# A 128-byte unused tile between the activation tiles and the weight tiles of a two-layer decoder trunk

## The chip, the cores and the metric

The kernel runs on one core of a Trainium2 chip. The metric is the device time of one execution in microseconds (us); lower is better.

## The reference

Two decoder layers work on 512 tokens of width 1024 in float32. Each has three sub-layers, each with a normalisation before and after it and a residual sum:

```
for l in range(DEPTH):
    h = hybrid_mixer(rmsnorm(x, pre_mix_g[l]), ...)          # dilated attention + mLSTM, one w_in, one w_out
    x = x + rmsnorm(h, post_mix_g[l])
    h = memory_cross_attention(rmsnorm(x, pre_mem_g[l]), mem, wq, wk, wv, wo)
    x = x + rmsnorm(h, post_mem_g[l])
    h = conv_ffn(rmsnorm(x, pre_ffn_g[l]), w_up, conv_w, conv_b, w_down)   # 1024 -> 2*2816 -> 1024
    x = x + rmsnorm(h, post_ffn_g[l])
```

Nearly all the arithmetic is in the products of activations with weights: w_in, w_out, the four projections of the cross-attention, w_up and w_down.

## The kernel before

**Split products.** Every float32 operand of a large product is split into a high and a low part (`split` L93, `load_unit` L84), and a product is three matmuls (`mm3` L108): high by high, high by low, low by high. Each matmul loads one stationary operand of 128 columns (512 bytes per partition) and streams a moving operand past it, mostly 512 columns (2,048 bytes per partition), into one accumulator in PSUM. Each matmul in the program has a weight load of its own, which the trace shows as PEld.

**The operands.** Weights come in units of 128 x 1024. `load_unit` brings a unit by DMA into `raw` (2 buffers), ScalarE rounds it to `whi` (L89) and VectorE puts the rest into `wlo` (L90); `whi` and `wlo` have 5 buffers of 4,096 bytes per partition each. Activations in feature order lie in big tiles `B` of 128 x 4 x 512 (8 buffers of 8,192 bytes, `bt` L61): two for the high parts and two for the low parts of one normalised input, so that `act(k)` (L260) gives one 2,048-byte row of each.

**The stages that use them.**
- `feat_gen` (L156) and `feat_halves` (L167): the weights are stationary and `B` moves. They do q, k and the convolved columns of the mixer, the q projection of the cross-attention and the whole up-projection of the MLP. `feat_halves` does the first four units of a stage in halves of 256 columns.
- `tok_gen` (L184): `B` is stationary and the weights move. It does the v, vm and om columns, w_out and wo. The same function with the tiles `mem` in place of `B` makes the values of the cross-attention (`fill_v` L359); `fill_k` (L345) makes the keys with `mem` moving, 256 columns wide.
- `down` (L985): the gated products are split into `gh` and `gl` (128 x 512, 4 buffers each), which are stationary, and the units of w_down move.

**Order.** PE's instructions stay in the order in which the program writes them (L42). Side tasks (attention, mLSTM, norms, transposes) are spliced into that order by `spawn` and `tick` (L115 to L127) with waiting times in `PACE` (L35), which count an estimated time of PE's matmuls (`mm` L99). All weight loads are issued on SyncE's queue.

**Where tiles lie.** The pool `pp` gives every tag its buffers when the tag is first called, one behind the other, each rounded up to 32 bytes; pools opened later (`mix`, `att`, `cross`, `ffn`, `mlstm`, `tail`) begin behind `pp`. In the order of the calls, and in bytes per partition, behind the eight `B` (L372) come: `gain` 2 x 4,096; three tags of one-column statistics, `ss` 8 x 32, `v` 8 x 32, `rstd` 4 x 32; `xg` 4 x 2,048; `raw` 2 x 4,096; `whi` 5 x 4,096; `wlo` 5 x 4,096; `tri` and `mask` 512 each; `mx`, `den`, `v0`, `dn` 4 x 32 each; `v4` 2 x 32. `ffn` begins with `fcw` (44 x 4 x 4 = 704 bytes); all else in it is a multiple of 2,048. `ident`, `x0` to `x3`, `ones` and the small per-layer weights `gw0`, `gw1` lie ahead of `B`. Every address below therefore stands modulo 512:

| tiles | start modulo 512 |
|---|---|
| `B` | 96 |
| `whi`, `wlo`, `raw`, `xg` | 224 |
| `gh`, `gl` (pool `ffn`) | 480 |
| `mem` | 256 or 288 |
| `k`, `qh`, `ql`, `v` of the cross-attention | 288 |
| `kh`, `kl`, `qa`, `ph`, `pl` of the attention | 32 in layer 0, 0 in layer 1 |
| `ident` | 128 |

The slices that a matmul takes of `B`, `whi`, `wlo`, `gh` and `gl` begin at multiples of 512 bytes within the tile, so the table holds for each of their operands.

Of the kernel before, what the change touches and what calls it, by code (L numbers as in the profile page):

```python
# [10 lines left out]
F32 = mybir.dt.float32  # L11
# [27 lines left out]
def trunk_kernel(ctx: ExitStack, tc: tile.TileContext, x4, memt, w, gw, gains, mcw, fcw, gb,  # L39
# [5 lines left out]
    pp = ctx.enter_context(tc.tile_pool(name="pp", bufs=1))  # L45
# [5 lines left out]
    def nm(s):  # L51
        uid[0] += 1
        return f"{s}_{uid[0]}"
# [7 lines left out]
    def bt(dt=F32):  # L61
        return pp.tile([128, 4, 512], dt, tag="B", name=nm("B"), bufs=8)
# [307 lines left out]
    nmu_d = [dr.tile([16, 128], F32, name=f"nmu_d{l}") for l in range(L)]  # L370

    xn = [bt(F32R) for _ in range(4)]  # L372
    grow = pp.tile([1, D], F32, tag="gain", name="grow", bufs=2)

    def load_x(t):
# [755 lines left out]
```

## Time and profile before

| | us |
|---|---|
| median of 3 runs | 1615.66 |
| lowest and highest of them | 1613.95, 1617.82 |
| the profiled execution's own time | 1615.79 |
| span of its trace | 1614.0 |
| PE busy, share of the span | 1595.4, 99% |
| VectorE (DVE) busy | 949.8, 59% |
| ScalarE (ACT) busy | 780.2, 48% |

The profile is one execution of the kernel. PE is a matmul, PEld a weight load, which lies beside a matmul. The duration of one matmul in the trace runs over the next one's start, since matmuls are pipelined; the pace of a stream of matmuls is read from the starts, that is, from a piece of the chain (its length by its count) or from the count in a window. Windows and pieces are given in us from the start of the span.

### The profile page before, as it was taken

Reading aid. Unit: us, or ns where it says so; the run is one execution under the profiler, and the core shown is the slowest. Engines: PE = TensorE matmul, PEld = TensorE weight load, DVE = VectorE, ACT = ScalarE, POOL = GpSimd, SP = SyncE. Lnnn points to the kernel's source line nnn. Section 1 sums busy time; section 2 is a strip of 40 time slices with the busy share of each in tenths; the row PEclk is TensorE's granted clock in tenths of the full one; section 3 lists DMA queues with packets and bytes.
Section 4 is the critical chain, followed back from the end, with each engine's and each line's share of the span. In section 5 each row is a group of like instructions: output and inputs, shape, how many; then the busy total and the mean of one; then the engine's idle time right before and its main releaser. Section 6 shows DMA issues by size and latency. Waiting matters only on the chain.

```text
span 1614.0 us, 21066 instructions
## 1 busy us (share of the span) xinstructions
PE 1595.4 (99%) x8032; PEld 1329.7 (82%) x8032; DVE 949.8 (59%) x1664; ACT 780.2 (48%) x1354; POOL 64.9 (4%) x92
## 2 busy tenths in 40 slices
PE   7999999999999999999999999999999999999998
PEld 5788888988798888888887888889888888888886
DVE  5687555746666555543376876557557655555334
ACT  5677574545554333333256775745445433333322
POOL 0000210000000000000010001101001000000000
PEclk9999999999999999999999999999999999999999
DMA  5422244551253222222323222445412322222221
GB/s 172 126 93 72 92 142 145 161 178 66 68 183 99 98 91 92 97 100 91 98 92 111 92 72 89 139 148 161 156 42 84 113 92 92 92 94 101 92 93 64
DMA packets 55414, 172.91 MB, mean 107 GB/s; under 512 B 6801, under 2 KB 9617, under 8 KB 55314
## 3 DMA queue, kind: packets, MB, share of 16 engines
q1 hardware_dynamic: 55314, 171.57, 32.6%
q8 instruction: 63, 1.03, 0.3%
q14 instruction: 37, 0.30, 0.1%
HBM read 165.22 MB, written 6.33 MB: 106 GB/s over the span
## 4 chain that ended last, share of the span: by engine, by line
PE 92%; DMA 2%; DVE 2%; ACT 2%; issue 1%; POOL 1%; SPq 0%; POOLq 0%; DVEq 0%; ACTq 0%
PE pg L102 75%; PE pa L102 14%; PE pa L106 3%; DMA raw<-in_w_dram 2%; DVE wlo L90 1%; ACT whi L89 1%; DVE xg L244 0%; POOL sq L629 0%; ACT junk L222 0%; DVE B L95 0%; DVE x L299 0%; DMA raw<-dv 0%; POOL sm L217 0%; DMA dk<-kf 0%; DMA raw<-dk 0%
## 5 line engine op out<-in xcount | busy, mean ns | idle before, releaser
L102 PE MATMUL pg<-B,whi 128*128 128x512 f32 (+1 forms) x2432 | 701.1, 374 | 1.4 <-DVE ql L924 1.4
L90 DVE TENSOR_TENSOR wlo<-raw,whi 128x1024 fp32r<-128x1024 f32 x268 | 328.9, 1228 | 297.0 <-ACT whi L89 293.6
L102 PEld LDWEIGHTS pg<-B,whi 128*128 128x128 f32 x2432 | 431.1, 188 | 77.3 <-DVE ql L924 1.6
L102 PE MATMUL pg<-B,wlo 128*128 128x512 f32 (+1 forms) x1216 | 451.0, 371 | 0.0
L89 ACT CAST whi<-raw 128x1024 fp32r<-128x1024 f32 x268 | 280.7, 1048 | 306.0 <-PE pg L102 239.1
L102 PE MATMUL pg<-whi,B 128*128 128x512 f32 x896 | 301.2, 402 | 0.0
L102 PEld LDWEIGHTS pg<-B,wlo 128*128 128x128 f32 x1216 | 228.7, 188 | 42.8
L102 PEld LDWEIGHTS pg<-whi,B 128*128 128x128 f32 x896 | 169.0, 189 | 38.1 <-DVE B L95 1.3
L102 PE MATMUL pg<-wlo,B 128*128 128x512 f32 x448 | 177.2, 395 | 0.6 <-DVE sm L236 0.6
L959 DVE SCALAR_TENSOR_TENSOR u<-pg,fcw,u 128x511 f32<-128x511 f32 (+1 forms) x176 | 131.5, 747 | 3.3
L102 PEld LDWEIGHTS pg<-wlo,B 128*128 128x128 f32 x448 | 84.8, 189 | 17.3 <-DVE wlo L90 1.0
L217 POOL TENSOR_TENSOR sm<-sm,mhalf 128x1 f32<-128x1 f32 x56 | 34.3, 612 | 1199.4 <-DVE sm L290 1022.7
L964 ACT ACTIVATE u<-u 128x512 f32<-128x512 f32 x44 | 27.8, 632 | 85.2 <-DVE u L959 85.2
L102 PE MATMUL pa<-whi,gh 128*128 128x512 f32 x176 | 68.7, 390 | 0.0
L102 PE MATMUL pg<-whi,gh 128*128 128x512 f32 x176 | 68.6, 390 | 0.0
L102 PE MATMUL pa<-wlo,gh 128*128 128x512 f32 x176 | 68.5, 389 | 0.0
L102 PE MATMUL pa<-whi,gl 128*128 128x512 f32 x176 | 68.5, 389 | 0.0
L102 PE MATMUL pg<-wlo,gh 128*128 128x512 f32 x176 | 68.5, 389 | 0.0
L102 PE MATMUL pg<-whi,gl 128*128 128x512 f32 x176 | 68.5, 389 | 0.0
L957 ACT ACTIVATE u<-pg,fcw 128x512 f32<-128x512 f32 x88 | 68.0, 773 | 0.0
L95 DVE TENSOR_TENSOR gl<-B,gh 128x512 fp32r<-128x512 f32 x32 | 22.2, 693 | 76.6 <-ACT gh L94 76.4
L94 ACT CAST gh<-B 128x512 fp32r<-128x512 f32 x32 | 19.9, 622 | 92.2 <-PE pg L102 87.1
(215 smaller groups left out, 1958.3 us busy)
## 6 DMA issues: line engine op xcount, KB each, us to landing
raw<-in_w_dram SPq DMA_DIRECT2D x268, 512.0 KB, 3.3
gain<-in_gains_dram SPq DMA_DIRECT2D x11, 512.0 KB, 3.6
raw<-in_memt_dram SPq DMA_DIRECT2D x20, 256.0 KB, 3.1
tb<-tb_d SPq DMA_DIRECT2D x16, 256.0 KB, 4.3
x<-in_x_dram SPq DMA_DIRECT2D x8, 256.0 KB, 5.7
e<-nmu_d SPq DMA_DIRECT2D x8, 256.0 KB, 3.8
dv<-vf SPq DMA_DIRECT2D x8, 256.0 KB, 2.7
dk<-kf SPq DMA_DIRECT2D x16, 128.0 KB, 4.1
```

What stands on the lines that cost most here:

```text
L89: ACT.copy(hi, raw)
L90: DVE.tensor_sub(lo, raw, hi.bitcast(F32))
L94: ACT.copy(hi, src)
L95: DVE.tensor_sub(lo, src, hi.bitcast(F32))
L102: PE.matmul(o, lhs, rhs, **kw)
L106: PE.transpose(o, src, idn)
L217: POOL.tensor_tensor(r, v, mhalf[:, :1], ALU.pow)
L957: ACT.activation(u, acc, AF.Identity, bias=fcw_t[:, m, 3:4], scale=fcw_t[:, m, 2:3])
L959: DVE.scalar_tensor_tensor(u[:, q:], acc[:, :512 - q], fcw_t[:, m, 2 - q:3 - q], u[:, q:], ALU.mult, ALU.add)
L964: ACT.activation(u, u, AF.Gelu_apprx_tanh)
```

## The change

One tile of 32 float32 per partition (128 bytes) is called from the pool `pp` between the first call of `B` and the first call of `gain`. No instruction reads or writes it. Every tile that is allocated behind it moves up by 128 bytes: `gain`, the statistics, `xg`, `raw`, `whi`, `wlo`, and all later pools. `B` and what lies ahead of it stay. Instructions, their order and their waits are the same.

```diff
     xn = [bt(F32R) for _ in range(4)]
+    pp.tile([128, 32], F32, name="pad")
     grow = pp.tile([1, D], F32, tag="gain", name="grow", bufs=2)
```

## Rows read from the trace of the kernel before

**Rows 1.** The page: span, busy time by engine, granted clock in 40 slices.

```profile
span 1614.0 us, 21066 instructions
...
PE 1595.4 (99%) x8032; PEld 1329.7 (82%) x8032; DVE 949.8 (59%) x1664; ACT 780.2 (48%) x1354; POOL 64.9 (4%) x92
...
PEclk9999999999999999999999999999999999999999
```

**Rows 2.** Chain that ended last, pieces by time: start us, length us, work, count.

```profile
264.08 16.75 PE pg L102 x72
...
838.30 11.89 PE pg L102 x51
...
499.79 204.73 PE pg L102 x881
...
707.26 2.72 PE pg L102 x12
709.98 2.72 PE pa L102 x12
```

**Rows 3.** Timeline of PE at 264 us and 714 us: start us, length us, instructions.

```profile
264.16 0.39 PE L102 MATMUL pg<-wlo,B 128*128 128x512 f32 x1
264.39 0.63 PE L102 MATMUL pg<-whi,B 128*128 128x512 f32 x2
264.85 0.40 PE L102 MATMUL pg<-wlo,B 128*128 128x512 f32 x1
...
714.12 0.39 PE L102 MATMUL pg<-wlo,gh 128*128 128x512 f32 x1
714.35 0.39 PE L102 MATMUL pg<-whi,gl 128*128 128x512 f32 x1
714.58 0.39 PE L102 MATMUL pg<-whi,gh 128*128 128x512 f32 x1
714.80 0.39 PE L102 MATMUL pg<-wlo,gh 128*128 128x512 f32 x1
```

**Rows 4.** Windows: stretch, length, busy us (count) of each engine, PEclk, DMA share, GB/s.

```profile
264.08:280.83 16.75, 16.75 (x74) 13.59 (x73) 8.45 (x15) 7.38 (x15) 0.00 (x0) 1.00 0.30 94
707.26:718.14 10.88, 10.88 (x49) 9.01 (x49) 5.31 (x7) 3.78 (x5) 0.00 (x0) 1.00 0.29 98
...
100.00:200.00 100.00, 99.72 (x516) 83.37 (x515) 74.57 (x163) 68.13 (x129) 9.95 (x10) 1.00 0.25 83
```

**Rows 5.** Groups of PE's matmuls by form and count: busy us, mean ns, idle before.

```profile
L102 PE MATMUL pg<-B,whi 128*128 128x512 f32 x1920 | 608.9, 398 | 1.4 <-DVE ql L924 1.4
L102 PE MATMUL pg<-B,wlo 128*128 128x512 f32 x960 | 379.0, 395 | 0.0
L102 PE MATMUL pg<-whi,B 128*128 128x512 f32 x896 | 301.2, 402 | 0.0
L102 PE MATMUL pg<-wlo,B 128*128 128x512 f32 x448 | 177.2, 395 | 0.6 <-DVE sm L236 0.6
L102 PE MATMUL pg<-B,whi 128*128 128x256 f32 x512 | 92.3, 283 | 0.0
L102 PE MATMUL pg<-B,wlo 128*128 128x256 f32 x256 | 72.1, 282 | 0.0
L102 PE MATMUL pa<-whi,gh 128*128 128x512 f32 x176 | 68.7, 390 | 0.0
...
L106 PE MATMUL pa<-ident,xg 128*128 128x128 f32 x192 | 29.7, 280 | 5.8 <-DVE xg L244 5.8
L106 PE MATMUL pa<-ident,s 128*128 128x128 f32 x160 | 27.7, 273 | 0.0
...
L102 PE MATMUL pa<-ph,B 128*128 128x256 f32 x64 | 16.9, 286 | 0.0
```

**Rows 6.** Chain that ended last: two pieces of 256-column matmuls, `mem` and `B` moving.

```profile
446.99 4.24 PE pg L102 x36
...
459.36 20.65 PE pg L102 x174
```

**Rows 7.** The page: shares of the chain by engine.

```profile
PE 92%; DMA 2%; DVE 2%; ACT 2%; issue 1%; POOL 1%; SPq 0%; POOLq 0%; DVEq 0%; ACTq 0%
```

**Rows 8.** Waits of PE after 12 us: us in total, times, longest us.

```profile
PE pg L102 <- DVE ql L924: 1.4, 1, 1.4
PE pa L102 <- DVE B L95: 1.0, 5, 0.3
```

## The prediction

> **What bounds the kernel now.** I read the page first: PE is busy for 99% of the span, VectorE for 59%, ScalarE for 48%, and the clock is granted in full from end to end [rows 1]. Nothing is to be had from another engine, so the question is how fast PE's stream of matmuls runs where it waits for nothing. The length of one matmul says little, because each runs into the next; the pace is in the starts. For that I read the chain's unbroken pieces and divide length by count [rows 2]:
>
> - weights moving, `B` stationary (w_out, 264 us): 16.75 / 72 = 232.6 ns
> - the same form in layer 1 (838 us): 11.89 / 51 = 233.1 ns
> - `B` moving, weights stationary (up-projection, 500 us): 204.73 / 881 = 232.4 ns
> - weights moving, `gh` and `gl` stationary (down-projection, 707 us): 2.72 / 12 = 226.7 ns, piece after piece
>
> All have 512 moving columns, 128 stationary columns and the same types. So two paces stand in one trace, 5.9 ns or 2.5% apart. The timeline shows the same between single starts: 0.23, 0.46 for two, and so on around 264 us, against a steady 0.23, 0.23, 0.22 around 714 us [rows 3].
>
> What sets them apart? First I asked whether it is load from the other engines. The windows say no: in the w_out piece VectorE is busy for 8.45 of 16.75 us and DMA moves 94 GB/s; in the down piece it is 5.31 of 10.88 us and 98 GB/s [rows 4]. That is 50% against 49%; ScalarE's 44% against 35% is the one visible difference. The form of the product is the same too: a 2,048-byte row of a weight unit moves past 512-byte slices of a stationary tile. What differs by the table of addresses is the distance of the operands modulo 512: `whi` is 128 above `B` (the 20 statistics slots between them are 640 bytes, and everything else is a multiple of 512), so 128 one way and 384 the other; `gh` is 256 above `whi` (64 bytes of `v4` and 704 of `fcw` make 768). A second difference is that `down` changes its accumulator every three matmuls and `tok_gen` mostly keeps one; the early part of `tok_gen`, which changes it every six, gives me no slower or faster piece, so I put this second.
>
> My reading: a weight load reads its 512 bytes while the matmul before it streams from the same memory, and at a distance of 128 or 384 the two disturb each other a little, at 256 less.
>
> **The change, part by part.** It adds no instruction, wait or DMA, and no queue is touched. It moves addresses.
>
> *Weights against `B`.* The distance goes from 128 to 256, in both roles: `whi` and `wlo` come to 352, `B` stays at 96. This is the pair of starts, 352 and 96, that the down stage's operands get as well. 512-column matmuls of the pair: 1,920 + 960 with `B` moving and 896 + 448 with weights moving, 4,224 in all [rows 5]. At 232.6 - 226.7 = 5.9 ns each that is 24.9 us. Not every one is followed by a weight load of its own pair: transposes and attention products are spliced in. The 192 and 160 transposes of the two largest groups come in groups of two to four [rows 5]; with the products I estimate 200 splices, 1.2 us. This term: **-23.7 us**.
>
> *The same pair at 256 columns* (`feat_halves`): 512 + 256 = 768 matmuls [rows 5]. The trace has none at a distance of 256, so I bound it. The pace now is 20.65 / 174 = 118.7 ns [rows 6]. One end is no gain; the trace gives that some support, since `mem` moving past weights, at another distance, runs at 4.24 / 36 = 117.8 ns [rows 6]. The other end is the whole 5.9 ns, 4.5 us. Between them: from 118.7 ns for 256 columns and 232.6 for 512, a matmul costs 4.8 ns fixed and 0.445 ns a column; if the fixed part stays and 226.7 ns is met at 512, 256 columns take 115.7 ns, 3.0 ns less. I take this, as it lies on the line through the rows for the same tiles: **-2.3 us**, ends 0 and -4.5.
>
> *The down stage, `mem`, and all pairs inside the later pools*: both partners move by 128, distances stay, 0.
>
> *Other pairs that change*: `B` stationary behind `ph`, `pl` in the attention, 64 `ph` matmuls of 256 columns [rows 5] and about as many `pl`; transposes of `xg` past `ident`. Less than 500 short matmuls; at up to 3 ns each, 1.5 us either way. I take 0.
>
> *VectorE, ScalarE, DMA*: the same work at addresses 128 bytes on. Their distance from PE's result to PE's next use is counted in PE's own work (`PACE`), so a PE that is 2% quicker reaches some waits earlier. The chain gives the size: it runs over PE for 92% of the span and over other engines for 8% [rows 7]. A faster PE gains nothing in the 8%, so of 26.0 us I take off 8%: **+2.0 us**. Ends: 0, since PE waits only 4.3 us in all after the start, the largest being 1.4 and 1.0 us [rows 8]; and 5 us, if the first wait of each kind doubles several times over. Next to be late would be the splits on VectorE that PE waits for there (`ql`, `B`).
>
> Sum: -23.7 - 2.3 + 2.0 = -24.0 us. Against the profiled execution's own 1615.79 us (span 1614.0 and 1.8 around it), which is within 0.2 us of the median of 1615.66, this gives **1592 us**.
>
> **A rule against it.** The trace has two paces for one form [rows 2]. The Trainium skill (TensorE: Matmul & The Clock Gate, section Step-by-step: what each phase is for) says that TensorE has two independent read ports and that "Loading the next tile's weights doesn't steal SBUF read bandwidth from the running matmul." By that sentence no address matters and the sum would be 0; the 5.9 ns speak against it as far as they are due to addresses, which this trace alone does not prove.
>
> **Rivals.**
>
> 1. *Nothing happens.* The gap is the accumulator's rotation in `down`, or ScalarE's share, or the unused tile takes no place. Weight loads and moving reads then do not meet, which is the rule above made into a mechanism. For: the down stage is the only place with 226.7. Against: 232 to 233 ns holds in both roles of `B` and at different loads. 1615.8 us, 7%.
> 2. *Only one role gains.* The row at 226.7 has weights moving; for `B` moving I argue by symmetry. If only the 1,344 with weights moving gain: 7.9 us less 0.6, 1608.5 us, 3%. If only the 2,880 with `B` moving: 17.0 + 2.3 less 1.5, 1598 us, 4%.
> 3. *The waits take it.* Side chains of fixed length become the bound outside the MLP: VectorE is at 75% in the mixer [rows 4]. If only the up-projection keeps its gain, 2 layers x 960 matmuls x 5.9 ns = 11.3 us: 1604.5 us, 3%.
> 4. *Slower.* The fast pace belongs to the start of `gh` itself (480) and not to a distance. The change moves `gh` to 96, the start of `B`, and the down stage falls to the pace of `B`: 2 x 528 = 1,056 matmuls (six groups of 176 [rows 5]) x 5.9 ns = 6.2 us, with nothing gained elsewhere: 1622 us. It decides from the moment that `down` runs at over 230 ns while w_out stays at 232. Against it: a start on its own means nothing to one reader, it needs a second to collide with. 3%.
>
> **How the numbers follow.** My forecast has 80%. Its own range: 24.9 + 4.5 us with nothing lost is 1586, and a pace 0.5 ns below 226.7, which the rows do not exclude, is 1584; with 5 us lost and no gain at 256 columns it is 1597. The range reaches on to the cases where only `B` moving gains and where the waits take the rest, to 1605; the cases left out (nothing, weights moving alone, slower) have 13%, and I leave some for the edges. A change below 0.2%, 3.2 us, can hardly be told from none in this kernel. Faster by more: 80 + 7 + 3 = 90%; within it: 7%; slower by more: 3%.
>
> **What would show it.** Right: pieces of the chain in w_out and in the up-projection at about 226.7 ns (12 matmuls in 2.72 us), the down stage unchanged at 226.7, 256-column pieces at 115 to 116 ns, PE still at 99% and its waits a few us longer. Wrong: the pieces stay at 232 (rival 1), `B` moving and weights moving part ways (rival 2), the pace falls but PE's idle time grows by over 5 us (rival 3), or the down stage slows (rival 4).

## The result and the profile after

The changed kernel takes 1598.66 us (median of four, 1597.46 to 1599.61) where the kernel before, in the runs taken with it, takes 1614.81: a ratio of 0.9898, 95% interval 0.9886 to 0.9910, that is 16 us or 1.0% faster. The forecast was 1592 us, the range 1584 to 1605. The direction and the place are as forecast, the size is two thirds of it.

The page after answers to [rows 1] and [rows 7]:

```profile
span 1596.5 us, 21066 instructions
...
PE 1576.7 (99%) x8032; PEld 1328.4 (83%) x8032; DVE 949.1 (59%) x1664; ACT 778.8 (49%) x1354; POOL 64.6 (4%) x92
...
PEclk9999999999999999999999999999999999999999
...
PE 87%; DMA 5%; DVE 4%; ACT 3%; issue 1%; POOL 1%; SPq 0%; POOLq 0%; DVEq 0%; ACTq 0%
```

As many instructions, the same clock, PE still at 99%: the busy time of PE itself fell by 18.7 us, that of the others by 1.4 at most. The chain's pieces after, by start us, length us, work and count, answer to [rows 2]; the last one, which the view cuts at its end, is of the w_out product of layer 1:

```profile
176.78 15.00 PE pg L102 x66
...
454.51 239.94 PE pg L102 x1146
694.46 2.72 PE pa L102 x12
697.18 2.72 PE pg L102 x12
...
1238.69 232.01 PE pg L102 x1080
...
1060.71 15.45 PE pg L102 x68
```

The same cuts of the chain before were these:

```profile
178.75 15.40 PE pg L102 x66
...
459.36 245.16 PE pg L102 x1146
...
1249.88 238.25 PE pg L102 x1080
```

What to see: the two up-projections, the same 1,146 and 1,080 matmuls, took 5.2 and 6.2 us less, 11.5 of the 17.5 us by which the span shrank. w_out runs at 15.45 / 68 = 227.2 ns, the vm columns of the mixer went from 233.3 to 227.3 ns, and the down stage, where both partners moved together, kept its 2.72 us for 12. But the short pieces between the mixer's side tasks gained less. First after, then before:

```profile
91.16 2.07 PE pg L102 x9
95.79 2.11 PE pg L102 x9
```

```profile
92.81 2.10 PE pg L102 x9
97.47 2.14 PE pg L102 x9
```

That is 230 and 234 ns against 233 and 238, 3 ns and not 6. PE's waits after 12 us answer to [rows 8]. Without the one for `xg` early in the run, which fell from 5.8 to 5.4 us, they grew from 4.3 to 5.9 us in all. The largest of them after:

```profile
PE pg L102 <- DVE ql L925: 2.2, 2, 1.5
PE pa L102 <- DVE B L95: 0.9, 5, 0.3
PE pa L106 <- ACT gs L443: 0.9, 1, 0.9
```

### The profile page after: what moved, and what is told of

Same layout as the page of the kernel before. It is cut to its first block, busy times and chain, and to the rows that moved or that the text cites. A ratio compares the mean times of both kernels' runs of the same rounds, so it can differ in the third digit from the quotient of the medians.

```text
span 1596.5 us, 21066 instructions
## 1 busy us (share of the span) xinstructions
PE 1576.7 (99%) x8032; PEld 1328.4 (83%) x8032; DVE 949.1 (59%) x1664; ACT 778.8 (49%) x1354; POOL 64.6 (4%) x92
## 4 chain that ended last, share of the span: by engine, by line
PE 87%; DMA 5%; DVE 4%; ACT 3%; issue 1%; POOL 1%; SPq 0%; POOLq 0%; DVEq 0%; ACTq 0%
PE pg L102 69%; PE pa L102 14%; PE pa L106 3%; DMA raw<-in_w_dram 3%; DVE wlo L90 1%; ACT whi L89 1%; DMA raw<-in_memt_dram 1%; DMA raw<-dv 1%; DVE xg L244 1%; DMA raw<-dk 1%; POOL sm L217 0%; ACT junk L222 0%; DVE x L299 0%; DMA dk<-kf 0%; POOL sq L630 0%
## 5 line engine op out<-in xcount | busy, mean ns | idle before, releaser
L102 PE MATMUL pg<-B,whi 128*128 128x512 f32 (+1 forms) x2432 | 693.4, 371 | 2.2 <-DVE ql L925 2.2
L102 PE MATMUL pg<-whi,B 128*128 128x512 f32 x896 | 297.5, 398 | 0.0
```

Source lines behind the costliest of these rows:

```text
L102: PE.matmul(o, lhs, rhs, **kw)
```

## The experiments

Three questions: is it the distance of the two operands that counts, or a start of its own, or something else that differs between the stages? How does the pace go with the distance? And why did the mixer gain so little? All distances are modulo 512, "forward" is the start of the next stationary operand less that of the moving one. Ratios are to the kernel before, run on the same chip.

### Distance, or place, or stage?

**All tiles moved together.** The unused tile goes one line up:

```diff
+    pp.tile([128, 32], F32, name="pad")
     xn = [bt(F32R) for _ in range(4)]
```

> The unused 128 bytes lie ahead of the B tiles, so B moves together with everything behind it: B 224, weights 352, gh 96 (modulo 512). The distances of B to weights (128) and of weights to gh (256) are those of the kernel before; only the distance to what lies ahead of B (ident, x, the gate weights) changes. Theory (the distance between the moving operand and the next stationary one sets the pace): 1615 us, within 2 us of the kernel before; up-projection at 232.5 ns a matmul, down stage at 226.7. Rival (the start of the weight tiles itself counts, 352 being a good one): 1598 to 1600 us, as with the changed kernel, 227 ns in the up-projection.

Measured: 1614.8 us, ratio 0.9994 (0.9984 to 1.0003). With the weights at 352 as in the changed kernel, but `B` 128 below them, nothing is gained. A start alone does nothing. The up-projection keeps its pace: the window from 500 to 600 us holds as many matmuls as before, but for two. First before, then here (length, then busy us and count for PE, PEld, DVE, ACT, POOL; the count takes in the matmuls that overlap either end):

```profile
500.00:600.00 100.00, 100.00 (x432) 81.06 (x431) 53.97 (x64) 37.27 (x46) 0.00 (x0) 1.00 0.29 95
500.00:600.00 100.00, 100.00 (x430) 80.46 (x429) 53.55 (x63) 37.41 (x46) 0.00 (x0) 1.00 0.29 95
```

**The weights and `B` left alone, the rest moved.** The unused tile lies behind the weights:

```diff
+    pp.tile([128, 32], F32, name="pad")
     tri = pp.tile([128, 128], F32, name="tri")
```

> The unused 128 bytes lie behind the weight tiles: B 96 and weights 224 as before (distance 128), gh and gl go from 480 to 96, so their distance to the weights goes from 256 to 128 the other way (384 forward). Theory (distance): the up-projection and w_out stay at 232.5 ns, the down stage falls from 226.7 to about 232.5 ns in 1,056 matmuls, 6 us slower: 1621 us (1619 to 1623). Rival (the down stage owes its pace to the change of accumulator every three matmuls or to the lighter load there): down stage stays at 226.7 and the time at 1615 us.

Measured: 1623.0 us, ratio 1.0038 (1.0024 to 1.0053), that is 6 us slower by the ratio, at the upper end of what was expected. The chain in the down stage:

```profile
710.90 2.79 PE pa L102 x12
713.69 2.79 PE pg L102 x12
```

2.79 / 12 = 232.5 ns: the pace of the down stage is lost with its distance, though the accumulator still changes every three matmuls and the load there is as light as it was (VectorE is busy for 34% of 720 to 790 us, 36% in the run before this one). `gh` lies at 96 here and at 96 in the changed kernel; with the weights 128 above it the pace is 232.5, with the weights 256 above it 226.7. This also answers rival 4.

### The pace against the distance

The same line as the change, with other sizes: 384 bytes (distance 0), 256 (384), 64 (192), 192 (320), 96 (224) and 160 (288).

```diff
     xn = [bt(F32R) for _ in range(4)]
+    pp.tile([128, SIZE // 4], F32, name="pad")
```

> The unused tile has 384 bytes in the place of the change: weights 96, B 96, distance 0; weights to gh stays 256. Theory (distance): the pace of the pair is that of distance 0, which the trace before shows only in the few ph-by-v matmuls of the cross-attention (about 228 to 229 ns for 512 columns); if that holds for a long stream the time lies between the two kernels, 1600 to 1606 us. If only 256 is good: 1615 us. If sameness of start is worst: above 1620 us.

Measured: 1598.95 us, ratio 0.9895 (0.9880 to 0.9911): the changed kernel over again, and better than the 1600 to 1606 us expected.

> The unused tile has 256 bytes in the place of the change: weights 480, B 96, distance 384; weights to gh stays 256. Theory (distance): 384 forward from B to weights is 128 from weights to B, the two roles only change places, so 232 to 233 ns in both and 1614 to 1617 us. Rival (any gap between B and the weights helps, or a larger one more): 1600 us or less.

Measured: 1615.05 us, ratio 0.9996 (0.9987 to 1.0005): the kernel before over again, as expected.

> The unused tile has 64 bytes: weights 288, B 96, distance 192 with B moving and 320 with weights moving; weights to gh stays 256. Four distances so far repeat after 256 (0 like 256, 128 like 384). Theory (two states, good only at a multiple of 256): 232 to 233 ns, 1613 to 1617 us. Rival (the pace falls off steadily between 256 and 128): about 229.5 ns, 1606 to 1609 us. Second rival (a quarter of the period has a pace of its own: with mem moved to a distance of 320 the 256-column matmuls of the keys ran at 114 to 115 ns and not at 118): faster than 226 ns in one of the two roles, below 1598 us if it is the one with B moving.

Measured: 1606.72 us, ratio 0.9947 (0.9931 to 0.9964), just between. It falls where the steady fall would have it, but the next three runs speak against that.

> The unused tile has 192 bytes: weights 416, B 96, distance 320 with B moving and 192 with weights moving, the mirror of the run with 64 bytes. Theory (two states): 1613 to 1617 us, 232 to 233 ns. Steady fall: 1606 to 1609 us. If a quarter of the period has its own pace, this run and the one with 64 bytes differ, since the roles change places: there are 2,880 matmuls of 512 columns with B moving and 1,344 with weights moving; the 256-column matmuls of the first units (B moving) should be at 114 to 115 ns here.

Measured: 1612.54 us, ratio 0.9977 (0.9968 to 0.9987). The up-projection gains nothing; w_out and the 256-column matmuls do, as shown below.

> The unused tile has 96 bytes: weights 320, B 96, distance 224 with B moving and 288 with weights moving, 32 bytes off the good distance. Theory (only a multiple of 256 lets the stream settle): 232 ns or more, since the values' matmuls with mem, 32 bytes off, run at 233 ns: 1614 to 1620 us. Rival (what counts is the distance to the nearest 128): close to the changed kernel, 1600 to 1603 us.

Measured: 1615.6 us, ratio 0.9996 (0.9986 to 1.0005), as expected.

> The unused tile has 160 bytes: weights 384, B 96, distance 288 with B moving and 224 with weights moving, 32 bytes off on the other side. Theory: 232 ns or more, 1614 to 1620 us. Rival (nearness to 256 counts): 1600 to 1603 us. If it differs from the run with 96 bytes, the sign of the distance matters and not only its size.

Measured: 1617.32 us, ratio 1.0010 (1.0000 to 1.0020), as expected.

One window shows the pace with `B` moving, the up-projection of layer 0 from 500 to 600 us, which held 432 matmuls before. For distances 256 (the change), 0, 384, 192, 320, 224 and 288 in this order:

```profile
500.00:600.00 100.00, 100.00 (x442) 82.78 (x442) 56.38 (x67) 37.47 (x47) 0.00 (x0) 1.00 0.29 96
```

```profile
500.00:600.00 100.00, 100.00 (x443) 82.84 (x442) 54.35 (x64) 38.39 (x48) 0.00 (x0) 1.00 0.31 100
```

```profile
500.00:600.00 100.00, 100.00 (x432) 81.08 (x431) 53.97 (x64) 37.32 (x46) 0.00 (x0) 1.00 0.29 95
```

```profile
500.00:600.00 100.00, 100.00 (x439) 82.04 (x438) 54.37 (x64) 37.81 (x47) 0.00 (x0) 1.00 0.30 100
```

```profile
500.00:600.00 100.00, 100.00 (x430) 80.55 (x429) 53.57 (x64) 37.18 (x46) 0.00 (x0) 1.00 0.28 95
```

```profile
500.00:600.00 100.00, 100.00 (x430) 80.36 (x429) 53.57 (x64) 37.45 (x46) 0.00 (x0) 1.00 0.29 95
```

```profile
500.00:600.00 100.00, 100.00 (x431) 80.55 (x430) 53.52 (x64) 37.36 (x46) 0.00 (x0) 1.00 0.29 95
```

What follows: 0 is like 256 and 128 like 384, so as far as these two pairs show the pace repeats after 256 bytes. Of the distances run, only the multiples of 256 give the full gain; 32 bytes beside 256, on either side, there is none. And the sign counts. A forward distance of 192 gives 439, its mirror 320 gives 430. When the roles change places, the good side does too: in w_out with weights moving, the run with 192 bytes (forward 192) has pieces of 7.57 us for 33, the run with 64 bytes (forward 320) 7.70, and the changed kernel 7.53.

```profile
1063.75 7.57 PE pg L102 x33
```

```profile
1057.45 7.70 PE pg L102 x33
```

```profile
1052.75 7.53 PE pg L102 x33
```

So of "two states" and "steady fall" neither held: the curve has one full optimum, one half optimum at 192 on one side only, and no gain at the other distances run. The second rival of the run with 64 bytes was right that the two roles part ways at a quarter distance, and wrong that one of them would be faster than 226 ns.

The 256-column matmuls have another curve. One stretch of 18 us in the first units of the up-projection, `B` moving, for the kernel before, the changed one and the one with 192 bytes:

```profile
462.92 18.15 PE pg L102 x153
```

```profile
457.99 18.12 PE pg L102 x151
```

```profile
462.94 18.13 PE pg L102 x160
```

118.6, 120.0 and 113.3 ns. The distance that is best for 512 columns is the worst of the three for 256, and over the whole stage the worst of all that were run.

### Why the mixer gains less

To bring the mixer's pattern into the MLP, 40 splices of four transposes are put into each up-projection, at a distance of 128 and of 256:

```diff
         for i in range(first, 2 * NF):
             run(feat_gen(l, U_UP + i, act, up_done(i // 2, i % 2)))
+            pd = pa()
+            for j in range(4):
+                PE.transpose(pd[:, 128 * j:128 * j + 128], ident, ident)
```

> The kernel before (distance 128) with four transposes of ident into a fresh accumulator, read by nobody, behind every unit of the up-projection from the fifth on: 40 splices in each layer. Theory (the stream at a distance of 128 has no settled state): a splice costs its own time, about 0.44 us as the transposes in the mixer do, 80 x 0.44 = 35 us, so about 1650 us, and the matmuls between splices keep their 232.5 ns. It is the counterpart of the next run.

> The changed kernel (distance 256) with the same 80 splices. Theory (the good pace of 226.7 ns is a state into which a stream settles some ten matmuls after anything else has run, which is why the mixer gained less than the MLP): the first matmuls of each unit run at 229 to 232 ns and the last at 226.7, about 228 on average, and the lead over the run with splices at a distance of 128 shrinks by 80 x 0.03 = 2 to 3 us, from 16 to 13 or 14 us. Rival (the mixer gained less because VectorE and ScalarE are busier there): these units, with the light load of the MLP, stay at 226.7 ns from the first matmul on, and the lead stays at 16 us.

Measured: 1649.62 us at 128, as expected, ratio 1.0215 (1.0198 to 1.0232), and 1634.35 us at 256, ratio 1.0124 (1.0108 to 1.0139). The lead is 15.3 us by the medians and 14.7 by the ratios; with intervals of 0.3% that cannot tell 13.5 from 16. The trace can tell whether the first matmuls behind a splice are slow. This is the timeline of PE at 256, one unit between two splices:

```profile
499.52 0.60 PE L986 MATMUL pa<-ident 128*128 128x128 f32 x4
499.87 0.71 PE L102 MATMUL pg<-B,whi 128*128 128x512 f32 x2
500.42 0.40 PE L102 MATMUL pg<-B,wlo 128*128 128x512 f32 x1
500.66 0.62 PE L102 MATMUL pg<-B,whi 128*128 128x512 f32 x2
501.12 0.39 PE L102 MATMUL pg<-B,wlo 128*128 128x512 f32 x1
501.35 0.62 PE L102 MATMUL pg<-B,whi 128*128 128x512 f32 x2
501.81 0.40 PE L102 MATMUL pg<-B,wlo 128*128 128x512 f32 x1
502.04 0.62 PE L102 MATMUL pg<-B,whi 128*128 128x512 f32 x2
502.50 0.39 PE L102 MATMUL pg<-B,wlo 128*128 128x512 f32 x1
502.73 0.62 PE L102 MATMUL pg<-B,whi 128*128 128x512 f32 x2
503.18 0.39 PE L102 MATMUL pg<-B,wlo 128*128 128x512 f32 x1
503.41 0.62 PE L102 MATMUL pg<-B,whi 128*128 128x512 f32 x2
503.86 0.39 PE L102 MATMUL pg<-B,wlo 128*128 128x512 f32 x1
```

Read the starts of the `wlo` rows, three matmuls apart: 500.42, 501.12, 501.81, 502.50, 503.18, 503.86. The first three steps are 0.70, 0.69, 0.69 us, 230 to 233 ns a matmul, the next ones 0.68, 227 ns. The stream needs nine or ten matmuls after a splice before it reaches the good pace. The starts behind all 80 splices say the same. The first matmul behind a splice takes 314 ns to the next start, 316 in the run at 128. Then the mean gap is 232.5 ns for the second to the fourth matmul, 230.4 for the fifth to the seventh, 228.6 for the next three, and 226.7 from the eleventh on. Over 226.7 ns that is 34 ns a splice, or 2.7 us for all 80, the loss that was expected. At 128 nothing settles: the gaps alternate between 229 and 237 ns up to the next splice. The rival fell: the load here is that of the MLP, and the first matmuls are slow all the same.

The changed kernel shows it with its own splices. Of its 232 unbroken runs of 512-column matmuls with `B` and weights, 181 are three, six or nine long, so they rarely get there. By place in its run, and without gaps that hold a wait, the first four matmuls gained nothing (231.6 ns before and after), the fifth to the tenth went from 232.8 to 228.9, and all later ones from 232.8 to 226.7.

**One partner in three.** Another 128 unused bytes between the tags `whi` and `wlo` (in `load_unit`, once):

```diff
+        if not padded:
+            padded.append(pp.tile([128, 32], F32, name="pad2"))
         lo = pp.tile([128, 1024], F32R, tag="wlo", name=nm("wlo"), bufs=5)
```

> The changed kernel with another 128 unused bytes between the whi and the wlo tiles: whi keeps its distance of 256 to B, wlo goes to 384, and gh, gl come to 128 the other way from whi and to 256 from wlo. Theory (each pair of a moving operand and the next weight load counts by itself): in the up-projection one pair of three is disturbed, in the down stage two of three, and neither settles: 230 to 232 ns in both, time between the two kernels or a little above, 1608 to 1620 us. Rival (the relation of the tiles of one product, hi parts only, sets the state): the up-projection stays at 226.7 ns and the down stage goes to 232: about 1605 us.

Measured: 1613.52 us, ratio 0.9993 (0.9984 to 1.0003). The up-projection has 434 matmuls in the window from 500 to 600 us, two above the kernel before and eight below the changed one; the down stage goes at 2.75 us for 12, 229 ns. The window and the chain's piece of 1,146:

```profile
500.00:600.00 100.00, 100.00 (x434) 81.84 (x433) 54.51 (x65) 37.31 (x46) 0.00 (x0) 1.00 0.29 95
...
459.31 244.04 PE pg L106 x1146
```

One pair of three off the good distance leaves the up-projection 1.1 of its 5.2 us (245.16 before, 239.94 in the changed kernel); the down stage, with two of three off, runs at 229 ns, a little better than the 230 to 232 expected. The starts tell why one pair costs so much. In unbroken streams with `B` moving, the gap in which `wlo` is loaded has a mean of 232.5 ns, the next one, in which `wlo` is in use, 234.1, and the third, with `whi` in use and `whi` loaded, keeps 226.8. There one pair at a bad distance slows two gaps. But the pairs do not simply count one by one: with weights moving, where `wlo` streams in one matmul of three, all three gaps are slow, 231.5 to 233.4 ns, and in the down stage the three stand at 232.5, 225.9 and 228.3. For the full gain all partners of a stream must have the distance; how the pairs act together stays open. The rival, by which the high parts alone set the pace, fell.

**Other pairs.** To the changed kernel, unused tiles ahead of `mem` in its pools and ahead of `k` in the cross-attention:

```diff
     def pool_mem(tp, off=32):
+        tp.tile([128, off], F32, tag="mempad", name=nm("mempad"))
         return lambda: tp.tile([128, 8, NM], F32R, tag="mem", name=nm("mem"), bufs=2)
...
-            box.append(mem_tiles(pool_mem(ml)))
+            box.append(mem_tiles(pool_mem(ml, 40)))
...
         q_tile(1)
+        cp.tile([128, 48], F32, name=nm("kpad"))
```

> The changed kernel with three more unused tiles, which put other pairs where the runs so far had their best pace: mem goes from 32 or 64 above the weights to 64 below them (modulo 256), so that the keys' matmuls (256 columns, mem moving, 384 of them) should go from 118 to 114.5 ns and the values' (512 columns, weights moving, 192) from 233 to 229; k of the cross-attention goes 64 below qh (256 columns, 192 matmuls) from 118 to 114.5 or a little more, since they run in groups of six. 1.3 + 0.8 + 0.5 us: 1596 us, 2 to 3 us below the changed kernel. If the quarter distance helps only long streams: 1597 to 1598 us.

Measured: 1596.53 us, ratio 0.9886 (0.9871 to 0.9901). The keys' matmuls gained what was expected; the same 42 of them in the changed kernel and here:

```profile
447.98 4.95 PE pg L102 x42
```

```profile
448.09 4.78 PE pg L102 x42
```

117.9 against 113.8 ns. The other pairs gained less than expected, by the starts: the values' matmuls went from 233.0 to 230.7 ns and not to 229, those of `k` past `qh` and `ql` from 118.3 to 117.4 and not to 114.5. The median is 2.1 us below that of the changed kernel, but the intervals of the two ratios overlap: the pieces are faster, the total is not shown to be. It is the lowest median of the study.

## Why the prediction was right, and where it was off

The starts of all matmuls, matched one to one between the two traces (the order of PE's instructions is the same), divide the 17.4 us between the first and the last of them. A gap is the time from one matmul's start to the next one's. One that is more than 60 ns over its columns at 2.4 a ns is counted as a wait.

| term | predicted, us | measured, us |
|---|---|---|
| `B` and weights, 512 columns | -23.7 | -18.9: 3,846 gaps, mean 232.6 to 227.7 ns |
| the same, 256 columns | -2.3 | +0.9: 751 gaps, mean 118.7 to 119.9 ns |
| waits and the chain off PE | +2.0 | +0.9 |
| all else | 0 | -0.4 |
| sum | -24.0 | -17.4 |

**What bounds the kernel**: right. PE's pace was the bound and still is.

**The two paces and their cause**: right, and now shown. The distance between the moving operands and the stationary ones decides: a common shift does nothing, a shift of one partner takes the down stage's pace away, the sizes give a curve in that distance, and moving `wlo` alone slows the up-projection's gaps in which `wlo` is loaded or in use and leaves the third as it was. Rival 1 has fallen with that. The prediction's "a weight load reads its 512 bytes while the matmul before it streams from the same memory" is more than was shown. That the two reads collide in the memory is what this looks like, but no run here sees the memory, and whether the stationary operand in use or the one loaded meanwhile counts more is open too.

The Trainium skill (TensorE: Matmul & The Clock Gate, Step-by-step: what each phase is for) has loading the next tile's weights take no read bandwidth from the running matmul. If that were all, the distance of the two would not matter; here a distance of 128 in place of 256 costs 232.5 - 226.7 = 5.8 ns a matmul.

**The 512-column term**: the mechanism was right, the size was off. The step that failed is "5.9 ns each", with a splice costing only its own gap: "I estimate 200 splices, 1.2 us". Where the stream is unbroken the price was exact: up-projection 232.4 to 226.7. But each splice also slows up to nine further gaps, and that is where 3.8 of the 4.8 missing us went: 3,846 gaps x (227.7 - 226.7) ns. By place in its run, the first four matmuls behind an interruption hold 2.8 us of that, the fifth to the tenth 1.0, and all later ones nothing. The other 1.0 is that fewer gaps than I took, 3,846 and not 4,020, are free of a splice and of a wait (174 x 5.9 ns).

**The 256-column term**: wrong in sign. I drew a line through 256 and 512 columns at one distance and moved it. The runs show no such line; each of the two widths has a curve of its own, and at a distance of 256 the short ones run at 119.9 ns. My bound of "no gain" excluded a loss without a reason.

**The waits**: +2.0 was taken from the chain's share off PE, 8%; measured were +0.9, inside the stated ends of 0 and 5. The wait for `ql`, named as the next to be late, grew from 1.4 to 2.2 us. A new one of 0.9 us was not foreseen: `gs`, the gate values of layer 1 that ScalarE evicts at L443, which now come after PE has reached their transposes. The chain's share off PE grew to 13%, but most of that is hidden, as PE's 99% shows.

**The rivals.** 2: both roles gained, 5.2 ns with `B` moving (232.7 to 227.5) and 4.3 ns with weights moving (232.4 to 228.1). Of those with `B` moving, 1,920 lie in the unbroken streams of the two up-projections; those with weights moving have no such stage. That makes the difference: behind the twelfth matmul of a run both roles stand at 226.7 ns. 3: real, but 1 us and not 12. 4: fell with the second run; `gh` now lies at 96 and keeps its 226.7.

**The range.** It held. That the time lies in its upper half is owed to two misses of the same sign, the splices and the 256-column matmuls, against one of 1 us the other way in the waits.

## What to carry to other kernels

When PE is at 99% and its stream has no waits, compare the pace of one form of matmul between stages, start to start; a difference of a few per cent between stages with the same shapes can come from nothing but the distance of the two operands in their partition. With 512 moving columns, try the stationary tiles a multiple of 256 bytes from the moving ones, all of them that one stream uses, and check it again when a tile is added to the pool between them; that was worth 2.5% of each unbroken stretch here. With 256 columns the same distance cost 1%. A price read from an unbroken stream is not the price in a stream that is interrupted every few matmuls.

## What the runs showed of the hardware that was not expected

- The pace has a memory. At a good distance a stream settles nine or ten matmuls after an interruption into gaps of 226 and 227 ns; at 128 it never does, and its gaps go round in a repeating pattern between 228 and 241 ns, with a mean of 232.8.
- The pace repeats after 256 bytes, as far as two pairs of distances show, and the sign counts: in unbroken streams a forward distance of 192 gives 228.9 ns a matmul in either role, 64 gives 233.3 in either.
- The best distance depends on the width. At 256 columns: 113 to 115 ns at a forward distance of 64 (modulo 256), 117.8 at 192, 118 to 119 at 128, 120 at 0. At 512 columns 0 is best.
- A tile that no instruction uses can cost time: one of 160 bytes in the place of the change made the kernel perhaps 0.1% slower (233.2 ns for `B` and weights in place of 232.6), and one of 128 bytes behind the weights slowed the down stage by 5.8 ns a matmul.
- Open: why a stream settles at all, how several pairs of one stream act together, and what it is that repeats after 256 bytes.
